# Three projections of a hybrid encoder layer: where the first one's column tiles and raw sums lie in SBUF, which queue loads them, and when its operands are split

## The chip, the cores and the metric

One core of one Trainium2 chip runs the whole layer. The metric is the device time of one execution in microseconds, the median of several runs; lower is better.

## The reference, cut to what matters

`x` is 512 tokens of 2048 channels. After RMSNorm, one input projection feeds two branches, an SSD scan and an attention over 16 heads. Each branch gives a 512 x 2048 array, `y` and `o`, and the layer ends with three 2048 x 2048 projections:

```python
o = bidir_attention(qn, qr, kn, kr, v) * jax.nn.silu(z_attn)
merged = jax.nn.sigmoid(g_ssm) * (y @ w_proj_ssm) + jax.nn.sigmoid(g_attn) * (o @ w_proj_attn)
return x + merged @ w_out            # float32 throughout, then a final RMSNorm
```

## The kernel before, in words

**Precision.** A float32 operand is split into a high part (`ACT` casts it to fp32r, L433) and a low part (`DVE` subtracts, L434); every product of two operands is three matmuls of 128 x 128 by 128 x 512 (high-high, low-high, high-low; L563, L564, L565).

**Strassen.** The projections `wps` (of `y`) and `wpa` (of `o`) use a 2 x 2 Strassen form, once for each half `cp` of the output columns. One half takes seven products, P1, P2, P5, P6, P3, P7, P4 in this order, of 48 matmuls each: four chunks `m` of weights (128 x 1024 f32, 512 KB each), and twelve matmuls a chunk. The operand side is one of x11, x12, S1, S2, S4, S3, x22 (`S1` to `S4` are sums of quarters of `y` or `o`); it is loaded raw in two halves of 512 KB (`raw_load`, L444, tile `xraw`) and split into a 16 KB-per-partition tile (`Ops.split`, `slot`). The weight side comes in tiles of three kinds: `wraw` (straight from `w`, three buffers, which the raw operand halves share), `X` and `Y` (four buffers each). X holds the "T1" column sums for P5, becomes X + Y for P6, and X + Y + `wraw` for P4; Y is P3's weight; "T3" sums, in Y buffers again, are P7's. T1 and T3 are made early by accumulating DMAs on POOL's queue.

**Who waits for whom.** A weight chunk is cast by ACT into `wh` and its rest written by DVE into `wl`, three buffers each, so the cast of chunk n waits until PE has done chunk n - 3. ACT, DVE, PE, and the queues of SP and POOL each work strictly in the order in which the scheduler of the program put them. PE's order is written by hand; those of the other engines follow the code order, moved forward by `high_priority(offset)` for loads (`LOAD_AHEAD`) and splits (`AHEAD`). `tc.keep_in_program_order` holds an instruction in code order.

**The stretch of the change.** In head 14 of the attention (`AH - 2`) `wps.head()` begins to be mixed into the heads: P1 and P2 of both halves of `wps` (called P1, P2, P1b, P2b) stand between the matmuls of heads 14 and 15. Before that the raw x11 and x12 of `y` are loaded and split into pool `xa`. When the last `pv` (probabilities by values, L168 to L170 on tile `op`) is written, pool `at` (attention tiles) closes and pool `xb` opens on the same memory, side "right", with `reuse_waits="tile"`: each new tile waits for the users of the bytes that it covers. In `xb` come five operand slots `opb` first, then four `Y`, then four `X`. The raw halves of S1 and S2 are put into `Y` tiles (loaded at L1477), the first T1 columns into `X` (L469), all on SP's queue. Then `wps.pair(0)`, `wps.pair(1)`, `wpa.pair(0)`, `wpa.pair(1)` run. `hooks` say after which product the next operand is loaded (`L`), split (`C`), or a step of the sums of `o` is issued on POOL's queue (`o_sums`: copies L1310, accumulates L1313). `done_ps` writes results to `ms_d` on POOL's queue (L1351), `fetch_ps` loads gates there (L1341).

Of the kernel before, what the change touches and what calls it, by code (L numbers as in the profile page):

```python
# [29 lines left out]
AH = 16  # L30
# [39 lines left out]
LOAD_AHEAD = 160  # L70


def build(tc, a):
    nc = tc.nc
    act, dve, pool, pe = nc.scalar, nc.vector, nc.gpsimd, nc.tensor
# [259 lines left out]
    class Fill:  # L335
# [43 lines left out]
    fill = Fill()  # L379
# [50 lines left out]

    def split_into(hi_, lo_, raw, sign=1):
        if sign == 1:
            act.copy(hi_, raw)  # L433
            dve.tensor_sub(lo_, raw, hi_.bitcast(F32))  # L434
# [12 lines left out]
    class Ops:  # L447
# [5 lines left out]
        def load(self, which):  # L453
            self.raws[which] = [raw_load(self.src[which], q) for q in range(2)]

        def split(self, which, op):
            for q, t in enumerate(self.raws.pop(which)):
                ks = slice(4 * q, 4 * q + 4)
                split_into(op[:, 0, ks], op[:, 1, ks], view4(t), -1 if which == "S2" else 1)
            self.view[which] = lambda s, j, i: op[:, s, j, i * P:(i + 1) * P]  # L460

    def w_load(t, w, cp, kh, cb, m):
# [1 line left out]
            nc.sync.dma_start(t, a[w][cp, kh, cb, m])  # L464
        return t

    def t_load(t, w, cp, name, m):
        with tc.high_priority(offset=LOAD_AHEAD):
            nc.sync.dma_start(t, t_d[w, cp, name][:, m * 1024:(m + 1) * 1024])  # L469
# [32 lines left out]
    def w_split(raw):  # L502
# [3 lines left out]
            split_into(h, l, raw)  # L506
        return h, l

    def w_tile(tag):
        with tc.high_priority(offset=LOAD_AHEAD):  # L510
            if tag == "w":
                return wp.tile([P, 1024], F32, tag="wraw", bufs=3, name="wraw")
            return cols.tile([P, 1024], F32, tag=tag, bufs=4, name=tag)

    def sum_tile(tag):

# [53 lines left out]
    class Strassen:  # L570
# [38 lines left out]

        def first(self, cp, name):  # L610
# [142 lines left out]
    cols = part_ = wx  # L753
# [505 lines left out]
    def scores(hd, t):  # L1259
        qh, ql, kh, kl, stack, zt = qks[hd]  # L1260
        tk = slice(t * P, (t + 1) * P)
        s = pa("s")
        pe.matmul(s, qh[:, tk], kh, start=True, stop=False)
        pe.matmul(s, qh[:, tk], kl, start=False, stop=False)
        pe.matmul(s, ql[:, tk], kh, start=False, stop=False)
        pe.matmul(s, stack[:, tk], kra, start=False, stop=False)
        pe.matmul(s, stack[:, tk], krb, start=False, stop=True)
        mx, nm, sm_ = (hi.tile([P, 1], F32, tag=n, bufs=4, name=n) for n in ("mx", "nm", "sm_"))
        dve.tensor_reduce(mx, s, AX.X, ALU.max)
        dve.tensor_scalar_mul(nm, mx, -SCALE)  # L1270
        pr = at_t("pr")
        act.activation(pr, s, AF.Exp, bias=nm, scale=SCALE, accum_out=sm_)
        dve.reciprocal(sm_, sm_)
        dve.tensor_scalar_mul(pr, pr, sm_)
        heads[hd][2][t] = pr
        if background and t == 1:
            pool.tensor_mul(pace, sm_, sm_)
            in_background(4)
# [107 lines left out]
    def o_sums(n, i=1):  # L1386
        return lambda: [tc.keep_in_program_order(f()) for f in o_late[i][n]]
# [27 lines left out]
    def some(n):  # L1415
        owed[0] += n
        owed[0] -= fill.run(owed[0])

    for hd in range(AH):
        pt_h = at.tile([P, TT, SEQ], F32R, tag="pt_h", bufs=2, name="pt_h")  # L1420
        pt_l = at.tile([P, TT, SEQ], F32R, tag="pt_l", bufs=2, name="pt_l")
        heads[hd] = (pt_h, pt_l, {})
        fill.until(("qk", hd))
        unit = 2.77 if hd < AH - 2 else 2
        scores(hd, 0)
        if hd:
            some(unit)
            trans(hd - 1, 3)
        some(2 * unit)
        scores(hd, 1)  # L1430
        some(3 * unit)
        if hd == AH - 2:
            fill.all()
            owed[0] = 0
            close_pool("ap")
            xa = part_ = open_pool("xa", reuse_waits="tile")
            for w in ("x11", "x12"):
                y_ops.load(w)
                y_ops.split(w, slot(w))
            kk = kp_  # L1440
            used.extend([0, 0, 3])
            fill.add("head", wps.head())
        if hd:
            pv(hd - 1)
        if hd == 12:
            for step in sums(o_d, slice(0, 1024)):
                for f in step:
                    f()
        trans(hd, 0)
        if hd == AH - 1:  # L1450
            o_sums(2, 0)()
        scores(hd, 2)
        some(3 * unit)
        trans(hd, 1)
        if hd == AH - 2:
            o_sums(0, 0)()
        some(2 * unit)
        scores(hd, 3)
        some(3 * unit)
        trans(hd, 2)  # L1460
        some(3 * unit)
        if hd >= AH - 2:
            o_sums((1, 3)[hd - AH + 2], 0)()
    some(8)
# [2 lines left out]
    pv(AH - 1, pb)  # L1467
    close_pool("at")
    xb = cols = open_pool("xb", side="right", reuse_waits="tile")
    xb.tile([P, 2, 8, 256], F32R, tag="opb", bufs=5, name="place")  # L1470
    for w, ahead_ in (("S1", LOAD_AHEAD), ("S2", 0)):
        if w == "S2":
            fill.all()
        with tc.high_priority(offset=ahead_):
            y_ops.raws[w] = [cols.tile([P, 1024], F32, tag="Y", bufs=4, name="xraw") for q in range(2)]
            for q in range(2):
                nc.sync.dma_start(y_ops.raws[w][q], yn_d[w][:, q * 1024:(q + 1) * 1024])  # L1477
# [160 lines left out]
```

## Time and profile before

| | |
|---|---|
| median of 3 runs (lowest, highest) | 2049.49 us (2048.11, 2053.45) |
| the profiled execution: its time, its span | 2056.61 us, 2054.8 us |
| mean granted TensorE clock in it | 0.985 |
| busy share of the span: PE, DVE, ACT, POOL | 96%, 71%, 47%, 15% |
| bytes moved by DMA | 378.56 MB, mean 184 GB/s |

The profile is one execution. A row of a timeline is: start in us, length, engine (SPq, POOLq or ACTq where its sequencer issues a DMA), line, operation, output<-inputs, shapes, count, and in brackets the idle time before it and what ended that. A row of the windows view gives, for each engine, the busy time in a stretch and the number of instructions that touch it (x), then the granted clock, the share of the 16 DMA engines that was busy, and GB/s. An unbroken stretch of PE in the Strassen products holds 44 to 45 matmuls in 10 us.

### The profile page before, as it was taken

Reading aid. Unit: us, or ns where it says so; the run is one execution under the profiler, and the core shown is the slowest. Engines: PE = TensorE matmul, PEld = TensorE weight load, DVE = VectorE, ACT = ScalarE, POOL = GpSimd, SP = SyncE. Lnnn points to the kernel's source line nnn. Section 1 sums busy time; section 2 is a strip of 40 time slices with the busy share of each in tenths; the row PEclk is TensorE's granted clock in tenths of the full one; section 3 lists DMA queues with packets and bytes.
Section 4 is the critical chain, followed back from the end, with each engine's and each line's share of the span. In section 5 each row is a group of like instructions: output and inputs, shape, how many; then the busy total and the mean of one; then the engine's idle time right before and its main releaser. Section 6 shows DMA issues by size and latency. Waiting matters only on the chain.

```text
span 2054.8 us, 24705 instructions
## 1 busy us (share of the span) xinstructions
PE 1970.9 (96%) x9074; PEld 1628.3 (79%) x9074; DVE 1466.0 (71%) x1946; ACT 968.1 (47%) x1352; POOL 318.0 (15%) x337
## 2 busy tenths in 40 slices
PE   6999999999999999999999989999999999999998
PEld 5878888888878787777788878888877777888886
DVE  7976676676669789799686667667576888776342
ACT  6444445444444656546456344444344454443232
POOL 0001011010032252342321101110010211100110
PEclk9999999999999999999999999999999999999999
DMA  5467657657457747687464856883377876865332
GB/s 196 164 179 202 171 127 194 183 120 188 134 174 193 222 142 207 195 237 230 145 189 146 241 161 180 211 220 95 85 207 257 293 251 258 264 227 169 109 117 82
DMA packets 166585, 378.56 MB, mean 184 GB/s; under 512 B 16001, under 2 KB 65281, under 8 KB 165889
## 3 DMA queue, kind: packets, MB, share of 16 engines
q1 hardware_dynamic: 104688, 238.33, 35.2%
q0 software_dynamic: 26944, 92.29, 20.5%
q10 hardware_dynamic: 34832, 46.38, 6.3%
q8 instruction: 71, 1.16, 0.2%
q14 instruction: 50, 0.40, 0.1%
HBM read 325.03 MB, written 98.04 MB: 206 GB/s over the span
## 4 chain that ended last, share of the span: by engine, by line
PE 72%; DVE 12%; DMA 7%; issue 5%; ACT 3%; POOL 1%; SPq 0%; ACTq 0%; DVEq 0%; POOLq 0%
PE P L564 10%; PE P L565 10%; PE P L563 10%; PE f L1507 3%; PE f L1508 3%; PE f L1506 3%; PE za L168 2%; PE za L169 2%; PE za L170 2%; PE xbc L168 2%; PE xbc L169 2%; DVE sum L1009 2%; PE xbc L170 2%; DVE wl L164 1%; DMA wraw<-wps 1%
## 5 line engine op out<-in xcount | busy, mean ns | idle before, releaser
L434 DVE TENSOR_TENSOR wl<-X,wh 128x1024 fp32r<-128x1024 f32 x152 | 185.4, 1223 | 82.4 <-ACT wh L433 81.7
L164 DVE TENSOR_TENSOR wl<-wraw,wh 128x1024 fp32r<-128x1024 f32 (+2 forms) x148 | 175.9, 1189 | 94.6 <-ACT wh L163 94.0
L433 ACT CAST wh<-X 128x1024 fp32r<-128x1024 f32 x152 | 159.4, 1053 | 155.6 <-PE P L565 135.8
L163 ACT CAST wh<-wraw 128x1024 fp32r<-128x1024 f32 (+2 forms) x150 | 145.0, 968 | 146.2 <-PE za L169 40.2
L434 DVE TENSOR_TENSOR wl<-wraw,wh 128x1024 fp32r<-128x1024 f32 x74 | 91.4, 1235 | 95.4 <-ACT wh L433 95.2
L434 DVE TENSOR_TENSOR wl<-Y,wh 128x1024 fp32r<-128x1024 f32 x80 | 98.0, 1225 | 76.4 <-ACT wh L433 76.4
L168 PE MATMUL xbc<-h_h,wh 128*128 128x512 f32 x384 | 152.4, 397 | 0.0
L170 PE MATMUL xbc<-h_h,wl 128*128 128x512 f32 x384 | 150.4, 392 | 0.0
L169 PE MATMUL xbc<-h_l,wh 128*128 128x512 f32 x384 | 150.3, 392 | 0.0
L564 PE MATMUL P<-wl,h_h 128*128 128x512 f32 x384 | 149.5, 389 | 0.0
L565 PE MATMUL P<-wh,h_l 128*128 128x512 f32 x384 | 149.5, 389 | 0.0
L563 PE MATMUL P<-wh,h_h 128*128 128x512 f32 x384 | 149.5, 389 | 0.0
L433 ACT CAST wh<-wraw 128x1024 fp32r<-128x1024 f32 x74 | 77.9, 1052 | 143.4 <-PE f L1508 68.6
L433 ACT CAST wh<-Y 128x1024 fp32r<-128x1024 f32 x80 | 83.9, 1051 | 113.9 <-PE P L565 91.4
L564 PE MATMUL P<-wl,S 128*128 128x512 f32 x288 | 112.5, 391 | 0.7 <-DVE wl L434 0.6
L563 PE MATMUL P<-wh,S 128*128 128x512 f32 x288 | 112.1, 389 | 0.0
L565 PE MATMUL P<-wh,S 128*128 128x512 f32 x288 | 112.1, 389 | 0.0
L168 PE MATMUL za<-h_h,wh 128*128 128x512 f32 x256 | 102.1, 399 | 0.0
L170 PE MATMUL za<-h_h,wl 128*128 128x512 f32 x256 | 100.7, 393 | 0.8 <-DVE wl L164 0.8
L169 PE MATMUL za<-h_l,wh 128*128 128x512 f32 x256 | 100.4, 392 | 0.0
L1009 DVE TENSOR_TENSOR_SCAN sum<-da,scn 128x512 f32<-128x512 f32 x64 | 87.3, 1382 | 0.0
L170 PEld LDWEIGHTS xbc<-h_h,wl 128*128 128x128 f32 x384 | 72.6, 189 | 15.6
(634 smaller groups left out, 5193.5 us busy)
## 6 DMA issues: line engine op xcount, KB each, us to landing
wraw<-wi SPq DMA_DIRECT2D x102, 512.0 KB, 4.1
T_wps<-wps POOLq DMA_DIRECT2D x32, 512.0 KB, 6.4
da<-da_d SPq DMA_DIRECT2D x64, 256.0 KB, 4.4
T_wpa<-wpa POOLq DMA_DIRECT2D x32, 512.0 KB, 9.5
wraw<-wo SPq DMA_DIRECT2D x32, 512.0 KB, 3.4
wraw<-wps SPq DMA_DIRECT2D x24, 512.0 KB, 4.8
xbc_d<-xbc ACTq DMA_DIRECT2D x24, 256.0 KB, 3.1
wraw<-wun SPq DMA_DIRECT2D x16, 384.0 KB, 3.1
```

The lines of the kernel that those rows point to most:

```text
L163: act.copy(h, raw)
L164: (dve if ahead[0] else pool).tensor_sub(l, raw, h.bitcast(F32))
L168: pe.matmul(out, wh, xh, start=start, stop=False)
L169: pe.matmul(out, wh, xl, start=False, stop=False)
L170: pe.matmul(out, wl, xh, start=False, stop=stop)
L433: act.copy(hi_, raw)
L434: dve.tensor_sub(lo_, raw, hi_.bitcast(F32))
L563: pe.matmul(bs[i], xh, wh, start=(j == 0), stop=False)
L564: pe.matmul(bs[i], xh, wl, start=False, stop=False)
L565: pe.matmul(bs[i], xl, wh, start=False, stop=(j == 7))
L1009: dve.tensor_tensor_scan(sums[dd], flat(da), mask, 0.0, ALU.add, ALU.mult)
L1506: pe.matmul(acc, mh, wh, start=(start and k == 0), stop=False)
```

## The change

1. **Pool `xb` has another order.** One slot (tag `opc`) first, then the four X tiles, then two tiles `Ya`, two tiles `Yb`, then four slots `opb`. X now covers the rotary query tile and the first `v_h` buffer, which the last `pv` does not use; `Yb` covers the first `v_l` buffer, also unused by then; `Ya` covers the second `v_h` buffer, which the last `pv` reads. S1's raw halves go to `Yb`, S2's to `Ya`.
2. **Eight loads change queue.** The first four T1 columns and the raw halves of S1 and S2 are issued on POOL's queue, not SP's.
3. **x12 of `y`** is loaded at the end of head 14 and split in head 15 code; it was loaded and split with x11.
4. **Operand splits of `o` move.** Each of x11, x12, S1, S2 of `o` is loaded and split one product later or more, its ACT cast pinned to code order (`CP`), and the steps of the sums of `o` are issued one or two products earlier.

```diff
 class Ops:
-        def split(self, which, op):
+        def split(self, which, op, in_order=False):
             for q, t in enumerate(self.raws.pop(which)):
                 ks = slice(4 * q, 4 * q + 4)
-                split_into(op[:, 0, ks], op[:, 1, ks], view4(t), -1 if which == "S2" else 1)
+                i = split_into(op[:, 0, ks], op[:, 1, ks], view4(t), -1 if which == "S2" else 1)
+                if in_order:
+                    tc.keep_in_program_order(i)          # i is the ACT cast
...
+    def col_tile(tag, name, dt=F32):
+        if tag == "Y" and cols is xb:
+            n_cols[0] += 1
+            return cols.tile([P, 1024], dt, tag=("Yb", "Ya")[(n_cols[0] - 1) // 2 % 2], bufs=2, name=name)
+        return cols.tile([P, 1024], dt, tag=tag, bufs=4, name=name)
...
+    def place(shape, name):
+        n = n_places[0] % 5
+        n_places[0] += 1
+        return xb.tile(shape, F32R, tag="opb" if n else "opc", bufs=4 if n else 1, name=name)
...
     wps = Strassen("wps", y_ops, -1, done_ps, fetch_ps, {
-        (0, "P5"): [C(y_ops, "S4"), L(y_ops, "S3"), o_sums(5, 0), o_sums(0)],
-        (0, "P6"): [C(y_ops, "S3"), L(y_ops, "x22"), o_sums(1)], (0, "P3"): [C(y_ops, "x22"), o_sums(2)],
-        (0, "P7"): [L(o_ops, "x11"), o_sums(3)], (0, "P4"): [C(o_ops, "x11"), L(o_ops, "x12"), o_sums(4)],
-        (1, "P5"): [C(o_ops, "x12"), L(o_ops, "S1"), o_sums(5)], (1, "P6"): [C(o_ops, "S1"), L(o_ops, "S2")],
-        (1, "P3"): [C(o_ops, "S2")], (1, "P7"): [L(o_ops, "S4")], (1, "P4"): [C(o_ops, "S4"), L(o_ops, "S3")]})
+        (0, "P5"): [C(y_ops, "S4"), L(y_ops, "S3"), o_sums(1)],
+        (0, "P6"): [C(y_ops, "S3"), L(y_ops, "x22"), o_sums(2)], (0, "P3"): [C(y_ops, "x22"), o_sums(3)],
+        (0, "P7"): [o_sums(4)], (0, "P4"): [L(o_ops, "x11"), o_sums(5)],
+        (1, "P5"): [CP(o_ops, "x11"), L(o_ops, "x12")], (1, "P6"): [CP(o_ops, "x12"), L(o_ops, "S1")],
+        (1, "P3"): [CP(o_ops, "S1"), L(o_ops, "S2")], (1, "P7"): [CP(o_ops, "S2"), L(o_ops, "S4")],
+        (1, "P4"): [CP(o_ops, "S4"), L(o_ops, "S3")]})
     wpa = Strassen("wpa", o_ops, -1, done_pa, fetch_pa, {
-        (0, "P1"): [C(o_ops, "S3"), L(o_ops, "x22")], (0, "P5"): [C(o_ops, "x22")],
+        (0, "P1"): [CP(o_ops, "S3"), L(o_ops, "x22")], (0, "P5"): [CP(o_ops, "x22")],
...
         scores(hd, 1)
+        if hd == AH - 1:
+            y_ops.split("x12", slot("x12"))
         some(3 * unit)
         if hd == AH - 2:
 ...
-            for w in ("x11", "x12"):
-                y_ops.load(w)
-                y_ops.split(w, slot(w))
+            y_ops.load("x11")
+            y_ops.split("x11", slot("x11"))
...
         some(3 * unit)
+        if hd == AH - 2:
+            y_ops.load("x12")
         if hd >= AH - 2:
             o_sums((1, 3)[hd - AH + 2], 0)()
...
     xb = cols = open_pool("xb", side="right", reuse_waits="tile")
-    xb.tile([P, 2, 8, 256], F32R, tag="opb", bufs=5, name="place")
-    for w, ahead_ in (("S1", LOAD_AHEAD), ("S2", 0)):
-        if w == "S2":
-            fill.all()
-        with tc.high_priority(offset=ahead_):
-            y_ops.raws[w] = [cols.tile([P, 1024], F32, tag="Y", bufs=4, name="xraw") for q in range(2)]
-            for q in range(2):
-                nc.sync.dma_start(y_ops.raws[w][q], yn_d[w][:, q * 1024:(q + 1) * 1024])
-        if w == "S1":
-            wps.first_columns(0)
-        C(y_ops, w)()
+    place([P, 2, 8, 256], "place")
+    wps.first_columns(0, pool)
+    for tag in ("Ya", "Yb"):
+        cols.tile([P, 1024], F32, tag=tag, bufs=2, name="place")
+    with tc.high_priority(offset=LOAD_AHEAD):
+        for w in ("S1", "S2"):
+            y_ops.raws[w] = [col_tile("Y", "xraw") for q in range(2)]
+            for q in range(2):
+                pool.dma_start(y_ops.raws[w][q], yn_d[w][:, q * 1024:(q + 1) * 1024])
+    CP(y_ops, "S1")()
+    fill.all()
+    CP(y_ops, "S2")()
     L(y_ops, "S4")()
     o_sums(4, 0)()
+    o_sums(5, 0)()
+    o_sums(0)()
     run(wps.pair(0, True))
```

PE's order is the same in both. What moves on the other engines, at three places (the number behind a name is a buffer's; `_213` and `_214` are S1 and S2 of `y`, `_216`, `_215`, `_212` are S4, S3, x22 of `y`, and `_217`, `_218` are x11, x12 of `o`):

SP's queue before, from the last head's value tile to the first pair (eleven `wraw` of P1, P2, P1b and P2b's first, then the S1 and T1 loads, then P2b's other three weights):

```order
L1226 DMA zt<-za_d_92 128x512
L464 DMA wraw<-wps 128x1024 x11
L1477 DMA xraw<-yn_S_213 128x1024
L469 DMA X<-T_wps_201 128x1024 x4
L1477 DMA xraw<-yn_S_213 128x1024
L464 DMA wraw<-wps 128x1024 x3
L1477 DMA xraw<-yn_S_214 128x1024 x2
L464 DMA Y<-wps 128x1024 x4
```

Three of P2b's four weights stand behind six transfers of 512 KB. SP's queue now, at the same place:

```order
L1239 DMA zt<-za_d_92 128x512
L467 DMA wraw<-wps 128x1024 x13
L467 DMA Y<-wps 128x1024
L445 DMA xraw<-yn_S_216 128x1024 x2
L467 DMA Y<-wps 128x1024
L445 DMA xraw<-yn_S_215 128x1024
L467 DMA Y<-wps 128x1024
```

All weights of P2b now stand in one row behind P1's, with nothing between; the Y loads are interleaved with the raw halves of S4 and S3.

POOL's queue now, from the last sum of `o` in the heads to the first results of `wps` (before, the first row was followed at once by `ms_d`):

```order
L1326 DMA o_S_222<-o_x_220 128x512
L472 DMA X<-T_wps_201 128x1024
L1507 DMA xraw<-yn_S_213 128x1024
L472 DMA X<-T_wps_201 128x1024 x3
L1507 DMA xraw<-yn_S_213 128x1024
L1507 DMA xraw<-yn_S_214 128x1024 x2
L1376 DMA ms_d_0_177<-p_13096 128x512
```

The eight loads stand between the last sum and the first result.

ACT before, from P3's weight casts (Y) to the eviction of the second half's P5 (`p`); `x__13529` is x22 of `y`, `x__13714` and `x__13814` are x11 and x12 of `o`:

```order
L433 CAST x__13529<-xraw 128x1024
L433 CAST wh<-Y 128x1024 x6
L433 CAST wh<-X 128x1024
L433 CAST x__13714<-xraw 128x1024
L433 CAST wh<-X 128x1024
L433 CAST x__13714<-xraw 128x1024
L433 CAST wh<-X 128x1024
L433 CAST x__13814<-xraw 128x1024
L433 CAST wh<-X 128x1024 x2
L433 CAST x__13814<-xraw 128x1024
L433 CAST wh<-X 128x1024 x5
```

Between two casts of P4's weights stands each time the cast of an operand half. ACT now, the same stretch and on to P3's casts of the second half (`x__13532` is x22 of `y`, `x__13808` and `x__13887` x11 and x12 of `o`):

```order
L433 CAST x__13532<-xraw 128x1024
L433 CAST wh<-Y 128x1024 x7
L433 CAST wh<-X 128x1024 x10
L539 COPY p_13804<-P_13718 128x512
L539 COPY p_13806<-P_13719 128x512
L433 CAST wh<-X 128x1024
L433 CAST x__13808<-xraw 128x1024 x2
L433 CAST wh<-X 128x1024
L433 CAST x__13887<-xraw 128x1024
L433 CAST wh<-Y 128x1024
L433 CAST x__13887<-xraw 128x1024
```

The four casts of `o`'s operands leave the row of P4's and P5's weight casts and now stand behind the second half's P5, the last of them behind the first Y cast of the second half's P3.

More of the change, by code (lines that the diff above doesn't have):

```diff
@@ L432, in split_into @@
         if sign == 1:
-            act.copy(hi_, raw)
+            i = act.copy(hi_, raw)
             dve.tensor_sub(lo_, raw, hi_.bitcast(F32))
         else:
-            act.activation(hi_, raw, AF.Copy, scale=-1.0)
+            i = act.activation(hi_, raw, AF.Copy, scale=-1.0)
             dve.scalar_tensor_tensor(lo_, raw, -1.0, hi_.bitcast(F32), ALU.mult, ALU.subtract)
+        return i
     def view4(t):
@@ L465, in w_load, with t_load @@
         return t
-    def t_load(t, w, cp, name, m):
+    def t_load(t, w, cp, name, m, queue=nc.sync):
         with tc.high_priority(offset=LOAD_AHEAD):
-            nc.sync.dma_start(t, t_d[w, cp, name][:, m * 1024:(m + 1) * 1024])
+            queue.dma_start(t, t_d[w, cp, name][:, m * 1024:(m + 1) * 1024])
         return t
@@ L507, in w_split @@
         return h, l
+    xa = xb = None
+    n_cols = [0]
+    def col_tile(tag, name, dt=F32):
[3 more added lines that the diff above has]
+        return cols.tile([P, 1024], dt, tag=tag, bufs=4, name=name)
     def w_tile(tag):
@@ L512, in w_tile @@
                 return wp.tile([P, 1024], F32, tag="wraw", bufs=3, name="wraw")
-            return cols.tile([P, 1024], F32, tag=tag, bufs=4, name=tag)
+            return col_tile(tag, tag)
     def sum_tile(tag):
@@ L598, in r_sum, with first_columns, columns @@
                 dve.scalar_tensor_tensor(out, x, -1.0, y, ALU.mult, ALU.subtract)
-        def first_columns(self, cp):
-            self.ahead[cp] = [self.columns(w_tile("X"), cp, m) for m in range(4)]
-        def columns(self, t, cp, m):
+        def first_columns(self, cp, queue=nc.sync):
+            self.ahead[cp] = [self.columns(w_tile("X"), cp, m, queue) for m in range(4)]
+        def columns(self, t, cp, m, queue=nc.sync):
             if self.made:
-                return t_load(t, self.w, cp, "T1", m)
+                return t_load(t, self.w, cp, "T1", m, queue)
             return w_load(t, self.w, cp, 0, 0, m)
@@ L1320, in build @@
             f()
-    xa = xb = None
+    n_places = [0]
+    def place(shape, name):
+        n = n_places[0] % 5
+        n_places[0] += 1
+        return xb.tile(shape, F32R, tag="opb" if n else "opc", bufs=4 if n else 1, name=name)
     def slot(which):
-        op_pool, tag, n = (xa, "opa", 2) if which in ("x11", "x12") else (xb, "opb", 5)
-        return op_pool.tile([P, 2, 8, 256], F32R, tag=tag, bufs=n, name=f"{which}_")
+        if which in ("x11", "x12"):
+            return xa.tile([P, 2, 8, 256], F32R, tag="opa", bufs=2, name=f"{which}_")
+        return place([P, 2, 8, 256], f"{which}_")
     y_ops, o_ops = Ops(yn_d), Ops(o_d)
@@ L1335, in C, with CP @@
         return lambda: ops.split(w, slot(w))
+    def CP(ops, w):
+        return lambda: ops.split(w, slot(w), True)
     fetched = {}
@@ L1378, in f @@
         def f():
-            t = mg[b] = xb.tile([P, 2, 4, SEQ], F32R, tag="opb", bufs=5, name="m")
+            t = mg[b] = place([P, 2, 4, SEQ], "m")
             for q, r_ in enumerate(m_raw.pop(b)):
@@ L1525, in last_load @@
             if i == 0:
-                last_w["op"] = xb.tile([P, 2, 2, 1024], F32R, tag="opb", bufs=5, name="keep")
+                last_w["op"] = place([P, 2, 2, 1024], "keep")
             h, l = (last_w["op"][:, i, s_] for s_ in range(2))
         else:
-            h, l = (xb.tile([P, 1024], F32R, tag=tag, bufs=4, name="keep") for tag in "XY")
+            h, l = (col_tile(tag, "keep", F32R) for tag in "XY")
         split_into(h, l, raw)
```

2 lines of the change are left out of this document (1 added, 1 removed).

## The prediction, made before the changed kernel ran

> **What bounds the kernel now.** I read the page first: PE is busy for nearly the whole span, and the chain that ended last is mostly PE.
>
> ```profile
> span 2054.8 us, 24705 instructions
> PE 1970.9 (96%) x9074; PEld 1628.3 (79%) x9074; DVE 1466.0 (71%) x1946; ACT 968.1 (47%) x1352; POOL 318.0 (15%) x337
> PE 72%; DVE 12%; DMA 7%; issue 5%; ACT 3%; POOL 1%; SPq 0%; ACTq 0%; DVEq 0%; POOLq 0%
> ```
>
> PE's matmuls and their order don't change, so the change can win or lose only time in which PE stands or runs at a lower clock. Up to 1490 us the queues are as they were; what counts is the stretch from there to the end of `wps`. The windows view cuts it so that stalled and unbroken stretches stand apart (per engine busy us and count, then clock, DMA share, GB/s).
>
> ```profile
> core 0: us, PE busy (x) PEld busy (x) DVE busy (x) ACT busy (x) POOL busy (x), PEclk, DMA share, GB/s
> 1490.00:1510.00 20.00, 20.00 (x99) 16.60 (x98) 12.77 (x27) 8.61 (x18) 3.68 (x5) 1.00 0.76 202
> 1510.00:1530.00 20.00, 15.69 (x58) 11.46 (x57) 15.48 (x26) 10.67 (x17) 1.37 (x2) 0.83 0.85 246
> 1530.00:1560.00 30.00, 30.00 (x144) 24.78 (x143) 19.17 (x34) 14.05 (x25) 0.80 (x1) 1.00 0.45 135
> 1570.00:1590.00 20.00, 15.71 (x62) 12.29 (x61) 11.62 (x10) 9.94 (x10) 0.00 (x0) 0.91 0.87 334
> 1590.00:1610.00 20.00, 20.00 (x90) 16.56 (x89) 19.07 (x20) 13.09 (x14) 4.62 (x8) 1.00 0.68 210
> 1610.00:1630.00 20.00, 17.78 (x76) 13.86 (x75) 15.89 (x18) 7.88 (x8) 1.68 (x2) 1.00 0.97 336
> 1640.00:1660.00 20.00, 16.14 (x59) 12.51 (x57) 15.51 (x17) 8.09 (x8) 3.09 (x5) 0.83 0.77 283
> 1700.00:1710.00 10.00, 7.04 (x28) 4.72 (x27) 7.05 (x8) 6.73 (x7) 3.21 (x6) 1.00 1.03 417
> 1710.00:1740.00 30.00, 30.00 (x134) 24.85 (x133) 28.07 (x27) 15.87 (x18) 2.14 (x4) 1.00 0.56 222
> ```
>
> An unbroken 20 us hold 99 matmuls in the heads (0.202 us each) and 90 in the pairs (0.222 us). What a stretch lacks of that is its loss, half clock included: 41 in the heads, 41 x 0.202 = 8.3 us; at 1570, 28 x 0.222 = 6.2; at 1610, 14 = 3.1; at 1640, 31 = 6.9; at 1700, 45 - 28 = 17 = 3.8. Together 28.3 us. After 1710 nothing is lost. So the change can bring at most 28 us, 1.4%.
>
> **Part 1, the first weights of P1 (8.3 us).** P1's first weights wait for the buffers that the raw x11 and x12 hold.
>
> ```profile
> 1508.72 2.00 ACT L433 CAST x__12693<-xraw 128x1024 fp32r<-128x1024 f32 x2
> 1513.73 1.59 SPq L464 DMA_DIRECT2D wraw<-wps  x2
> 1518.47 1.04 ACT L433 CAST wh<-wraw 128x1024 fp32r<-128x1024 f32 x1 [1.01 <-DMA wraw<-wps]
> 1519.56 0.50 PE L563 MATMUL P<-wh,x__12693 128*128 128x512 f32 x1 [2.32 <-ACT wh L433]
> 1520.82 0.80 PE L564 MATMUL P<-wl,x__12693 128*128 128x512 f32 x1 [0.76 <-DVE wl L434]
> ```
>
> With x12 later, two weight loads follow x11's halves directly and their casts stand ahead of x11's, so both waits of PE go: 2.32 + 0.76 = 3.1 us. The half clock goes with them: 0.83 over 20 us is 17% of 20 = 3.4 us. The other 8.3 - 6.5 = 1.8 us are waits for softmax pieces behind x11's split on ACT and DVE, which stays. x12's two casts (1.0 us each, as x11's in the first row) and its subtractions now fall between the weight casts of P1, with x12's second raw half waiting for x11's buffer; I expect 1.5 us of new waits there for a scaled score row ahead of a transpose. Gain 6.5 - 1.5 = 5.0 us, ends 3 and 8.
>
> The Trainium skill ("TensorE: Matmul & The Clock Gate", Part 1: The HAM clock gate) states that the clock falls to half after an idle window of some 3.4 us. By that rule the 2.32 and 0.76 us above would not have caused the half clock, and its 3.4 us would stay: the sum would be 3.4 us smaller. The trace shows the half clock right behind them, so the sum goes by the trace.
>
> **Part 2, the first pair's loads on POOL's queue (6.2 us).** At P2b everything arrives at once.
>
> ```profile
> 1530.12 0.80 POOL L1313 DMA_DIRECT2D o_S<-o_x  x1 [5.58 <-DMA o_S<-o_S]
> 1559.94 0.37 SPq L1477 DMA_DIRECT2D xraw<-yn_S  x1
> 1560.40 2.56 SPq L469 DMA_DIRECT2D X<-T_wps  x4
> 1561.58 0.60 POOL L1351 DMA_DIRECT2D ms_d<-p  x1 [30.65 <-DVE p L1350]
> 1563.89 11.92 DMA wraw<-wps
> 1574.53 1.04 ACT L433 CAST S__13064<-xraw 128x1024 fp32r<-128x1024 f32 x1 [3.17 <-DMA xraw<-yn_S]
> 1575.88 1.04 ACT L433 CAST wh<-wraw 128x1024 fp32r<-128x1024 f32 x1 [0.31 <-DMA wraw<-wps]
> 1576.98 0.49 PE L563 MATMUL P2b<-wh,x__12702 128*128 128x512 f32 x1 [3.53 <-ACT wh L433]
> ```
>
> P2b's second weight takes 11.92 us to land behind six 512 KB transfers, and ACT stands 3.17 us for S1 in front of it. Now the six leave SP. On POOL they come behind the sum at 1530.12, where POOL then idles 30.65 us; their tiles lie over bytes that the last heads no longer read, so they issue from about 1531 on, at 0.8 us each. The DMA engines are 45% busy there at 135 GB/s; they moved 336 GB/s at 0.97, so 30 us have room for 30 x 201 = 6.0 MB, and six times 0.524 MB is 3.1. What they could delay are P2's and P1b's weights, which are loaded some 10 us before use. S2's two raw halves wait for the last `pv` (PE, about 1556); behind them on POOL stand only `ms_d` of P2 at 1561.58 and its gates. SP loses eight issues of 0.4 us and no longer holds P2b's weights. Gain 6.0 of 6.2, ends 4 and 6.2. If POOL could not issue them before 1560, the 6.2 would stay.
>
> The Trainium skill ("DMA: Bandwidth & Descriptors", Issuing engines are not separate DMA queues) says that all queues run on the same 16 engines and another issuing engine saves only issue time. By that rule alone, with the loads still at 1560, this part would bring nothing and the sum 6.0 us less. The rows show that it is the place in time that changes, and no run so far shows the two apart.
>
> **Part 3, x22 ahead of P3 (3.1 us).** ACT stands for x22's second half with P3's weights queued behind it.
>
> ```profile
> 1603.01 2.77 SPq L444 DMA_DIRECT2D xraw<-yn_x  x2
> 1614.13 1.05 ACT L433 CAST x__13529<-xraw 128x1024 fp32r<-128x1024 f32 x1 [4.91 <-DMA xraw<-yn_x]
> ```
>
> This half was issued at about 1605.5 and took 8.7 us. Now S4 and S3 are cast during P5, but DVE's subtraction of S4's second half and of S3 stands behind the `wl` of P6's chunks, and those subtractions free x22's buffers. Working it through with PE unbroken, x22 issues at about 2.6 and 5 us after P6's start (before: 4.3 and 6.8), and only one Y cast, not two, stands ahead of its second half. With a landing of 4.7 us (the shortest row of part 4) nothing is lost; with 8.7 again some 3 us. DVE is full there (19.07 of 20 us in 1590 to 1610). I take 2.0 lost, gain 1.1, ends -1 and 3.
>
> **Part 4, operands of `o` out of P4 (6.9 us).** The two halves of x12 of `o` hold up P4's weight casts.
>
> ```profile
> 1634.01 9.76 DMA xraw<-o_x
> 1636.38 0.39 SPq L444 DMA_DIRECT2D xraw<-o_x  x1
> 1643.79 1.04 ACT L433 CAST x__13814<-xraw 128x1024 fp32r<-128x1024 f32 x1 [6.10 <-DMA xraw<-o_x]
> 1648.97 1.04 ACT L433 CAST x__13814<-xraw 128x1024 fp32r<-128x1024 f32 x1 [2.24 <-DMA xraw<-o_x]
> ```
>
> In the new order no operand cast stands between P4's: gain 6.9, ends 5 and 6.9. Three 512 KB loads (x12's second half, S1) also leave this saturated stretch. Against it: DVE now adds the last two `wraw` into X back to back ahead of P7's second `wl`, and the last of them waits for its buffer, 0.7 us; and x12's second half is now issued when x11's first is split, 4.8 us after P5 of the second half, while ACT reaches it 2.9 us later, with P3's second Y cast behind it and slack for a landing of 5.5 us; 0.7 us. Landings of half a megabyte in this trace go from 4.71 to 11.92 us.
>
> ```profile
> 1513.73 4.71 DMA wraw<-wps
> 1682.93 5.22 DMA wraw<-wps
> ```
>
> **Part 5, S4 and S3 of `o` ahead of the second P4 (3.8 us).** Here too ACT stands for operands with weights behind.
>
> ```profile
> 1700.03 1.05 ACT L433 CAST S__14164<-xraw 128x1024 fp32r<-128x1024 f32 x1 [5.45 <-DMA xraw<-o_S]
> 1705.09 1.05 ACT L433 CAST S__14251<-xraw 128x1024 fp32r<-128x1024 f32 x1 [3.06 <-DMA xraw<-o_S]
> ```
>
> Now S4's casts stand behind five X casts and S3's behind the next product. But S2's halves keep two of three buffers until P7, so P4's third and fourth `wraw` are issued only when S2's halves are split, in P7, some 6 us before PE wants the third X; with the 5.22 us landing above, the addition and the cast behind it, that X is ready 0.9 us late. I take 2.0 lost, gain 1.8, ends -2 and 3.8.
>
> The sums of `o` on POOL move from under P6 to P4 to P2b to P7; the copies and accumulates are the same in number, none is waited for by the products of `y`, and they cost nothing but DMA share, which is counted in parts 3 to 5.
>
> **Sum.** 5.0 + 6.0 + 1.1 + 6.9 - 0.7 - 0.7 + 1.8 = 19.4 us. The profiled execution took 2056.6 us and would take 2037.2; the median of the runs is 7.1 us under it, so I forecast 2049.5 - 19.4 = 2030 us. The ends of the parts added are 3 + 4 - 1 + 5 - 0.7 - 0.7 - 2 = 7.6, and 27.9 with the two new waits at nothing.
>
> **Rivals.**
> - *Everything clears.* All landings are near 4.8 us because the burst at 1560 is gone and the sums are spread. Then 26 to 28 us go: 2022. For it: every stall stands in a stretch with a DMA share of 0.85 to 1.03. Against it: P3 and P7 still load seven half megabytes each in 11 us, 337 GB/s, about what full engines moved (336). Chance 0.15.
> - *DMA stays the bound.* Stalls in P3, P7 and both P4 come back, because the bytes are the same and the stretch is shorter. Parts 3 and 5 bring nothing, P7 and P4 lose 4 us: 19.4 - 1.1 - 1.8 - 4 = 12.5, or 2037. Chance 0.22.
> - *The loads do not move.* POOL's queue reaches them only behind a late sum, or P2's weights suffer as P2b's did: 2030 + 6 = 2036. The 30.65 us speak against it. Chance 0.05.
> - *Slower: pinned casts wait in order.* Each pinned operand's second half is issued only when a buffer frees and ACT then stands for it. At P3, P7, P4 of the second half and at two products of `wpa` that is a stall of the landing less 5.5 us. At 9.8 us landing (the row at 1634) it is 5 x 4.3 = 21 us, and with half the time as half clock 5 x 1.7 = 8.5 more; parts 1 and 2 and P4 bring 18, so 12 us slower: 2061. It decides from landings of about 8.5 us at all five. Chance 0.04.
>
> **Numbers.** The forecast itself, 2024 to 2036, has the remaining 0.54. Range 2021 to 2041: it leaves out the slow side's tail and little below. 0.3% is 6.1 us, about what a measurement of this kernel can tell from no change (the three runs span 5.3). Faster by more than that: all of the 0.54, 0.15 and 0.05, and 0.17 of the 0.22 (its rest ends above 2043.4), 0.91, less a little for the tails, 0.90; within 0.3%: 0.06; slower: 0.04.
>
> **What would show it.** T1 columns and S1 issued by POOL between 1530 and 1540, and no wait of P2b for `wh` over 1 us; P1's first matmul directly behind the score matmuls, at clock 1.0; ACT without a wait for `xraw` of `o` among P4's casts; a wait left at P3 or the second P4 of 1 to 3 us. Wrong would be: a wait of ACT of over 4 us for the x12 half of `o` in the second half's P3, late P2 weights behind POOL's loads, or a loss in `wpa`.

## The result, and the profile after

The changed kernel took 2040.26 us (median of 5 runs, 2034.87 to 2043.42), the kernel before 2049.49 (2048.09 to 2058.72). The ratio is 0.9935, 95% interval 0.9913 to 0.9957: faster by 0.65%. Run again later beside other kernels it gave 0.9946 (0.9930 to 0.9961).

The first lines of the page of the changed kernel:

```profile
span 2033.1 us, 24719 instructions
PE 1955.8 (96%) x9074; PEld 1619.0 (80%) x9074; DVE 1465.7 (72%) x1946; ACT 967.4 (48%) x1352; POOL 324.7 (16%) x345
PE 72%; DVE 14%; DMA 6%; issue 4%; ACT 3%; POOL 1%; SPq 0%; ACTq 0%; DVEq 0%; POOLq 0%
```

The two profiled spans are 21.7 us apart, more than the medians, because the profiled execution of before lies 7.1 us above its median and that of the changed kernel (2034.87 us) 5.4 under it. At the first matmul of the last `pv` ahead of P1 the changed kernel is 10.4 us ahead already, in work that both do alike (1500.86 against 1511.26 us; other profiles with the changed kernel's order reach it at 1503 and at 1511). So the stretch from there on is compared: to the first matmul of `wpa` it took 188.25 us, before 199.80. That is 11.55 us less; behind it nothing differs (347.05 and 358.63 us to the end of `wpa`). The next lines are the windows view of the changed kernel, with the columns of the one shown of before.

```profile
1499.60:1519.60 20.00, 17.51 (x84) 13.42 (x83) 17.86 (x33) 12.88 (x22) 2.47 (x4) 1.00 0.81 250
1555.70:1566.60 10.90, 10.90 (x50) 9.01 (x49) 9.12 (x9) 9.25 (x10) 0.00 (x0) 1.00 0.86 294
1566.00:1577.00 11.00, 11.00 (x50) 9.12 (x49) 10.17 (x11) 6.12 (x6) 1.07 (x2) 1.00 0.34 137
1588.00:1599.00 11.00, 11.00 (x50) 9.10 (x49) 10.71 (x12) 4.80 (x5) 1.68 (x2) 1.00 1.00 336
1599.00:1610.00 11.00, 6.91 (x23) 5.25 (x22) 7.17 (x9) 2.14 (x3) 1.54 (x3) 0.76 0.99 349
1628.00:1638.00 10.00, 10.00 (x46) 8.29 (x45) 9.56 (x11) 4.70 (x5) 3.10 (x5) 1.00 0.24 87
1671.00:1682.00 11.00, 7.15 (x29) 5.38 (x29) 7.04 (x7) 3.04 (x3) 1.07 (x2) 0.90 0.97 388
1682.00:1689.00 7.00, 7.00 (x23) 5.49 (x22) 6.04 (x9) 3.14 (x3) 2.14 (x4) 0.67 0.93 269
```

The heads run at clock 1.00 (0.83 before), and P2b (second row) is unbroken. But two stretches have holes in PE and a lower clock: 1599, which is P7 of the first half, and 1671, which is P4 of the second. In both the DMA engines are full, while at 1566 and 1628, three products before and two behind the first hole, they move 137 and 87 GB/s.

What PE waited for in P7 is seen in DVE's timeline:

```profile
1597.60 1.23 DVE L434 TENSOR_TENSOR wl<-Y,wh 128x1024 fp32r<-128x1024 f32 x1
1600.58 1.23 DVE L674 TENSOR_TENSOR X<-X,wraw 128x1024 f32<-128x1024 f32 x1 [1.75 <-DMA wraw<-wps]
1604.02 1.23 DVE L674 TENSOR_TENSOR X<-X,wraw 128x1024 f32<-128x1024 f32 x1 [2.21 <-DMA wraw<-wps]
1605.16 1.22 DVE L434 TENSOR_TENSOR wl<-Y,wh 128x1024 fp32r<-128x1024 f32 x1
```

The row at 1605.16 is the `wl` of P7's second chunk. Its `wh` was there at 1599; it stood behind two additions that P4 needs only a product later, each of which waited for a `wraw`. In P4 of the second half the additions themselves are late (ACT's timeline, then two rows of the chain):

```profile
1677.16 1.04 ACT L433 CAST wh<-X 128x1024 fp32r<-128x1024 f32 x1 [6.37 <-DVE X L674]
1679.56 1.99 ACT L433 CAST wh<-X 128x1024 fp32r<-128x1024 f32 x2 [1.35 <-DVE X L674]
```

```profile
1595.24 8.76 DMA wraw<-wps
1669.65 8.54 DMA wraw<-wps
```

Both `wraw` took over 8.5 us to land, where the rows shown in the prediction had 4.71 and 5.22.

### The profile page after: what moved, and what is told of

It reads as the page before. It is cut to its first block, busy times and chain, and to the rows that moved or that the text cites. A ratio compares the mean times of both kernels' runs of the same rounds, so it can differ in the third digit from the quotient of the medians.

```text
span 2033.1 us, 24719 instructions
## 1 busy us (share of the span) xinstructions
PE 1955.8 (96%) x9074; PEld 1619.0 (80%) x9074; DVE 1465.7 (72%) x1946; ACT 967.4 (48%) x1352; POOL 324.7 (16%) x345
## 4 chain that ended last, share of the span: by engine, by line
PE 72%; DVE 14%; DMA 6%; issue 4%; ACT 3%; POOL 1%; SPq 0%; ACTq 0%; DVEq 0%; POOLq 0%
PE P L577 10%; PE P L578 10%; PE P L576 10%; PE f L1539 3%; PE f L1540 3%; PE f L1538 3%; PE za L168 2%; PE za L169 2%; PE za L170 2%; PE xbc L168 2%; DVE sum L1022 2%; PE xbc L169 2%; PE xbc L170 2%; DVE wl L164 2%; DMA wraw<-wps 1%
```

## The experiments

Each product is read as the time from its first matmul to the next product's; one without a stall is 10.88 us. "Heads" goes from the first matmul of the last `pv` ahead of P1 to P1b, "all" from there to the end of `wpa`. "P4-P6'" are P4 and the second half's P5 and P6 (32.64 without a stall), "wpa P1-P2" the first four products of `wpa` (43.52).

| kernel | heads | P2b | P3 | P7 | P4-P6' | second P4 | wpa P1-P2 | all | ratio to before |
|---|---|---|---|---|---|---|---|---|---|
| before | 48.43 | 17.24 | 13.96 | 10.88 | 39.87 | 15.02 | 43.52 | 358.63 | |
| changed | 43.98 | 10.89 | 10.87 | 17.65 | 32.64 | 17.83 | 43.52 | 347.05 | 0.9935 |
| e8 (as e1) loads on SP | 44.37 | 20.48 | 12.71 | 12.12 | 32.64 | 16.53 | 43.52 | 352.43 | 0.9980 (e1) |
| e2 old places of `o` | 43.98 | 10.89 | 11.01 | 16.38 | 34.67 | 14.61 | 43.52 | 347.20 | 0.9940 |
| e3 additions late | 44.40 | 10.88 | 10.88 | 10.88 | 36.14 | 18.18 | 44.26 | 345.43 | 0.9943 |
| e4 sums later | 44.24 | 10.88 | 11.24 | 18.11 | 32.64 | 19.42 | 43.52 | 353.09 | 0.9967 |
| e5 S2 later | 46.80 | 10.88 | 11.12 | 18.22 | 32.64 | 10.88 | 47.64 | 348.55 | 0.9930 |
| e6 all later | 44.40 | 10.88 | 10.88 | 11.53 | 36.54 | 10.88 | 60.30 | 355.55 | 0.9974 |
| e7 x12 early | 47.26 | 10.88 | 10.88 | 16.37 | 32.64 | 18.23 | 43.52 | 349.49 | 0.9963 |
| e9 e3 and e5 | 44.98 | 10.88 | 10.88 | 11.30 | 34.88 | 10.88 | 44.93 | 338.46 | 0.9903 |
| e10 changed again | 44.49 | 10.88 | 10.91 | 16.40 | 32.65 | 17.96 | 43.52 | 346.65 | 0.9946 |
| e11 without adds | 43.54 | 10.88 | 10.94 | 13.85 | 32.64 | 17.60 | 43.52 | 343.51 | (one run) |

The ratios carry about 0.002 either way, 4 us, so single steps are read from the product times, and the ratio only says whether they add up. A product time is that of one profiled execution: in the four kernels with the changed kernel's order from P1b to P7 (changed, e5, e7, e10) P7 took 16.4 to 18.2 us, so differences under 2 us there say nothing.

**e1 and e8: the eight loads on SP's queue.**

```diff
-    wps.first_columns(0, pool)
+    wps.first_columns(0)
...
-                pool.dma_start(y_ops.raws[w][q], yn_d[w][:, q * 1024:(q + 1) * 1024])
+                nc.sync.dma_start(y_ops.raws[w][q], yn_d[w][:, q * 1024:(q + 1) * 1024])
```

> The changed kernel, with the eight loads (four T1 columns, S1, S2) on SP's queue again; tiles and places in the code as in the change. SP's order then has them behind P2b's first weight and ahead of its other three. Theory (the place in time decides, and POOL's queue is what gives it): SP reaches them only when the buffers of P1b's weights come free, some 15 us later than POOL does, so P2b's weights again land behind 4 MB: P2b stalls 4 to 6 us (none now), and the time is some 5 us above the changed kernel, ratio to the kernel before 0.996 to 0.998. Rival (the free tiles alone do it, another issuing queue saves only issue time): P2b stalls under 1 us, ratio 0.993 to 0.995 as the changed kernel.

Its ratio is 0.9980 (0.9966 to 0.9995), as the theory had it. Its product times come from e8, another execution of the same kernel:

> The first run's kernel again (the eight loads on SP's queue), one look, for its profile. Theory: X's first column is issued by SP some 15 us later than by POOL, P2b's wraw stand behind, and P2b takes 15 to 17 us (10.88 now). Rival: P2b takes under 12 us.

SP's timeline in e8, a row of its chain, and POOL's timeline in the changed kernel:

```profile
1538.73 11.70 SPq L467 DMA_DIRECT2D wraw<-wps  x4
1550.54 0.37 SPq L472 DMA_DIRECT2D X<-T_wps  x1
1556.60 3.61 SPq L467 DMA_DIRECT2D wraw<-wps  x3
```

```profile
1556.60 12.43 DMA wraw<-wps
```

```profile
1520.13 0.96 POOL L472 DMA_DIRECT2D X<-T_wps  x1
1521.24 2.21 POOL L472 DMA_DIRECT2D X<-T_wps  x3
1541.67 1.05 POOL L1507 DMA_DIRECT2D xraw<-yn_S  x2 [17.70 <-PE op L170]
```

The tiles are the same and equally free. SP comes to the first column 44.6 us behind the `pv` (1550.54 - 1505.91), POOL 19.3 us (1520.13 - 1500.86), because SP stands 11.70 us on weights whose buffers are not free. The next of P2b's `wraw`, behind the eight loads, then takes 12.43 us to land, and P2b 20.48 us. Freeing the tiles alone doesn't help; the theory holds, with a larger price in P2b than the 15 to 17 us expected. Of its 9.6 us only 5.4 are left at the end (352.43 - 347.05), mostly because P7 stalls 5.5 us less. DVE has the same order there as in the changed kernel, two additions ahead of the second `wl`, but the last `wraw` lands sooner:

```profile
1612.28 5.45 DMA wraw<-wps
```

**e2: parts 1 to 3 of the change alone**, with loads, splits and sums of `o` as before: the removed rows of the hooks in the diff of the change stand again, and

```diff
     o_sums(4, 0)()
-    o_sums(5, 0)()
-    o_sums(0)()
```

> The changed kernel with the loads, splits and sums of o where they were before (parts 1 to 3 of the change alone). Theory (moving o's operands only moved the stalls): P4 and the second P4 stall again for operand halves of o (6 and 3 us), but P7 of the first pair (6.8 us now) and the 6.9 us of the second P4 go down; in sum 0 to 4 us under the changed kernel, ratio to the kernel before 0.991 to 0.994. Rival (the move of o's operands earned its 6.9 us): about 5 us above the changed kernel, ratio 0.995 to 0.997.

0.9940 (0.9922 to 0.9959), and 347.20 us against 347.05: the move of `o`'s operands is worth nothing. Its stalls stand in other products: P7 loses 5.5 us and the second half's P5 to P7 1.1, 0.8, 1.2 and 0.8, where the changed kernel loses 6.8 in P7 and 3.2 us more in the second P4. The theory's sum came nearly true, but not its places: P4 does not stall again for operand halves (10.96 us), and P7 loses as much as in the changed kernel's other profile (5.5). DVE's timeline in e2 shows why P7 does:

```profile
1604.81 1.23 DVE L674 TENSOR_TENSOR X<-X,wraw 128x1024 f32<-128x1024 f32 x1 [2.29 <-DMA wraw<-wps]
1607.26 1.23 DVE L674 TENSOR_TENSOR X<-X,wraw 128x1024 f32<-128x1024 f32 x1 [1.23 <-DMA wraw<-wps]
1608.40 1.22 DVE L434 TENSOR_TENSOR wl<-Y,wh 128x1024 fp32r<-128x1024 f32 x1
```

The two additions stand ahead of P7's second `wl` here too, with the operands of `o` in their old places. That order of DVE came with parts 1 to 3, not with part 4; which of the three brings it isn't shown.

**e3: P7's last two additions behind its `wl`.**

```diff
-                t4(m, w_load(w_tile("w"), w, cp, 1, 0, m))
+                raw = w_load(w_tile("w"), w, cp, 1, 0, m)
+                t4(m, raw) if m < 2 else tc.keep_in_program_order(dve.tensor_add(X[m], X[m], raw))
```

> The changed kernel with one edit in P7: the third and fourth addition of wraw into X are held in code order, so DVE does them behind the wl of P7's chunks. Theory (P7 waits because the addition that waits for the last wraw stands ahead of the second chunk's wl): P7 of the first pair takes 11 to 12.5 us (17.65 now), that is 5 to 6.5 us less, ratio to the kernel before 0.990 to 0.992 if P4 doesn't take it back. Rival (DMA is the bound, T3's weights are late as well): P7 stays above 15 us, or P4 takes back what P7 wins, because X's third and fourth tile come late; ratio 0.993 to 0.995.

P7 takes 10.88 us: its 6.8 us were DVE's order alone, not late T3 weights. But 3.5 us come back in P4 to P6'. ACT's timeline in e3 shows it at P5 of the second half, for T1 columns:

```profile
1630.08 1.04 ACT L433 CAST wh<-X 128x1024 fp32r<-128x1024 f32 x1 [7.41 <-DMA X<-T_wps]
1631.94 1.05 ACT L433 CAST wh<-X 128x1024 fp32r<-128x1024 f32 x1 [0.82 <-DMA X<-T_wps]
```

The whole stretch gained 1.6 us (1.2 against e10), and the ratio (0.9943, 0.9924 to 0.9961) can't tell that from nothing. So both theories had a half.

**e4: sums of `o` issued from P4 on.**

```diff
-        (0, "P6"): [C(y_ops, "S3"), L(y_ops, "x22"), o_sums(2)], (0, "P3"): [C(y_ops, "x22"), o_sums(3)],
-        (0, "P7"): [o_sums(4)], (0, "P4"): [L(o_ops, "x11"), o_sums(5)],
+        (0, "P6"): [C(y_ops, "S3"), L(y_ops, "x22")], (0, "P3"): [C(y_ops, "x22")],
+        (0, "P7"): [], (0, "P4"): [L(o_ops, "x11"), o_sums(2)],
...
         (the second half's P5, P6 and P3 get o_sums(3), o_sums(4), o_sums(5))
```

> The changed kernel with steps 2 to 5 of the sums of o's second column half issued behind P4, and in P5, P6, P3 of the second half (before: behind P6 to P4 of the first). Theory of order on DVE: the last wraw of P7 lands 1 to 2 us earlier (8.76 us now), P7 still stalls 3 to 6 us, ratio 0.992 to 0.994. Rival (the accumulating DMAs fill the engines and are the cause): the landing falls to about 5 us, P7 stalls under 2 us, ratio 0.990 to 0.991. Against both: S2 and S4 of o could come late in the second half's P3 and P7 behind POOL's gates; then the second P4 stalls more than 7 us.

Neither, but the third case that was named: P7 takes 18.11 us with a landing of 8.74, and S2 comes later (its second raw half is issued 2.3 us ahead of the second half's P7, against 4.5 in the changed kernel), and the second P4 takes 19.42 us; 0.9967 (0.9954 to 0.9980). The landing in P7 is as slow without the later steps of the sums beside it.

**e11: the accumulating DMAs of those sums left out.**

```diff
-        return lambda: [tc.keep_in_program_order(f()) for f in o_late[i][n]]
+        return lambda: [tc.keep_in_program_order(f()) for f in (() if i and n % 2 else o_late[i][n])]
```

> The changed kernel without the accumulating DMAs of the sums of o's second column half (the copies stay, the sums are left out, so S1 to S4 of o hold only copies there). Theory (order on DVE and buffers make the two stalls; the accumulates are 1 of some 15 MB): P7 still stalls by 4 us or more and the second P4 by 5 or more. Rival (accumulating DMAs slow the loads beside them): P7 stalls under 2 us; the second P4, behind which no sum runs, stays as it is.

One row of its chain:

```profile
1597.86 7.24 DMA wraw<-wps
```

The landing falls to 7.24 us (8.76 and 8.17 in the two profiles of the changed kernel), and P7's stall to 3.0 us (6.8 and 5.5), between the two expectations; the second P4 stays (17.60). More than half of what P7 gains is that the clock stays at 1.00 behind the shorter hole (2.56 us; 4.09 and 3.58 there). In e3, with all sums in place, that landing was 7.67 us, so this one execution leaves open whether the accumulates cost P7 anything.

**e5: S2, S4, S3 and x22 of `o` one product later.**

```diff
-        (1, "P3"): [CP(o_ops, "S1"), L(o_ops, "S2")], (1, "P7"): [CP(o_ops, "S2"), L(o_ops, "S4")],
-        (1, "P4"): [CP(o_ops, "S4"), L(o_ops, "S3")]})
+        (1, "P3"): [CP(o_ops, "S1")], (1, "P7"): [L(o_ops, "S2")],
+        (1, "P4"): [CP(o_ops, "S2"), L(o_ops, "S4")]})
...
-        (0, "P1"): [CP(o_ops, "S3"), L(o_ops, "x22")], (0, "P5"): [CP(o_ops, "x22")],
+        (0, "P1"): [CP(o_ops, "S4"), L(o_ops, "S3")], (0, "P5"): [CP(o_ops, "S3"), L(o_ops, "x22")], (0, "P6"): [CP(o_ops, "x22")],
```

> The changed kernel with S2, S4, S3 and x22 of o each loaded and split one product later (S2 is loaded in the second half's P7 and split in its P4). Theory (S2's raw halves hold two of the three wraw buffers, so the last two wraw of the second P4 are issued too late): the second P4 takes 11 to 13 us (17.8 now), nothing comes back in the attention projection, ratio to the kernel before 0.990 to 0.992. Rival (full DMA engines, 0.97 there, are what makes the last wraw late): the second P4 stays above 15 us, ratio 0.993 to 0.995.

The second P4 takes 10.88 us. Its last `wraw` is now issued 10.9 us ahead of it, 1.6 in the changed kernel: S2's raw halves in the `wraw` buffers were the cause of the stall. 4.1 us come back in `wpa`'s first four products, 2.5 of them in its P5. ACT's timeline in e5 there:

```profile
1706.62 1.05 ACT L433 CAST wh<-X 128x1024 fp32r<-128x1024 f32 x1 [3.50 <-DMA X<-T_wpa]
1710.35 1.05 ACT L433 CAST wh<-X 128x1024 fp32r<-128x1024 f32 x1 [2.68 <-DMA X<-T_wpa]
```

The ratio (0.9930, 0.9904 to 0.9956) leaves both open. The theory's "nothing comes back" failed. In this profile the heads took 2.8 us more than in the changed kernel, with the same order there.

**e6: e3, and every operand of `o` one product later still.**

```diff
-        (0, "P7"): [o_sums(4)], (0, "P4"): [L(o_ops, "x11"), o_sums(5)],
...
+        (0, "P7"): [o_sums(4)], (0, "P4"): [o_sums(5)],
+        (1, "P5"): [L(o_ops, "x11")], (1, "P6"): [CP(o_ops, "x11"), L(o_ops, "x12")],
+        (1, "P3"): [CP(o_ops, "x12")], (1, "P7"): [L(o_ops, "S1")],
+        (1, "P4"): [CP(o_ops, "S1"), L(o_ops, "S2")]})
...
+        (0, "P1"): [CP(o_ops, "S2"), L(o_ops, "S4")], (0, "P5"): [CP(o_ops, "S4"), L(o_ops, "S3")], (0, "P6"): [CP(o_ops, "S3"), L(o_ops, "x22")], (0, "P2"): [CP(o_ops, "x22")],
```

> The late additions of the third run (P7's third and fourth addition behind its wl) and every operand of o one product later still: x11 is loaded in the second half's P5 and split in P6, S2 is split after the attention projection's P1. Theory (each stall left is a load that meets a burst, and moving 1 MB of x11 out of the first P4 and S2 out of the second P7 thins both): P7 of the first pair and the second P4 take 11 to 12.5 us, the waits of P4, P5 and P6 for T1 columns in the third run (3.5 us) go below 2, ratio 0.986 to 0.989. Rival (the bytes only come back elsewhere): over 4 us of new stalls, in the second half or in the attention projection, ratio 0.991 to 0.994.

0.9974 (0.9955 to 0.9992). P7 and the second P4 are nearly clean and T1 columns are still waited for, but `wpa`'s P6 and P2 lose 4.2 and 12.5 us. SP's timeline there:

```profile
1711.80 2.59 SPq L445 DMA_DIRECT2D xraw<-o_x  x2
1716.21 24.29 SPq L467 DMA_DIRECT2D wraw<-wpa  x5
```

x22's halves now hold two of the three `wraw` buffers while P2 wants them for its weights, so P2's loads go one by one for 24 us. The rival's new stalls came, larger than it had them (its ratio was 0.991 to 0.994), and by buffers, not by bytes.

**e7: x12 of `y` loaded and split beside x11**, as before.

```diff
-            y_ops.load("x11")
-            y_ops.split("x11", slot("x11"))
+            for w in ("x11", "x12"):
+                y_ops.load(w)
+                y_ops.split(w, slot(w))
```

> The changed kernel with x12 of y loaded and split beside x11, as before. Theory: P1's first weights wait again for x12's raw buffers, and the heads from the last but one pv to P1b take 47 to 49 us (43.98 now, 48.43 before); ratio to the kernel before 0.995 to 0.997. Rival (the 4.5 us came from elsewhere, the loads on POOL's queue or noise of the half clock): the heads stay at 44 to 45 us, ratio as the changed kernel, 0.992 to 0.995.

Two rows of PE's timeline in e7, and a row of its windows view:

```profile
1510.84 0.49 PE L576 MATMUL P<-wh,x__12693 128*128 128x512 f32 x1 [2.31 <-ACT wh L433]
1512.10 0.50 PE L577 MATMUL P<-wl,x__12693 128*128 128x512 f32 x1 [0.77 <-DVE wl L434]
```

```profile
1510.00:1530.00 20.00, 18.39 (x81) 14.95 (x82) 14.69 (x27) 10.46 (x18) 5.39 (x9) 0.91 0.93 264
```

The same two waits as before the change (2.32 and 0.76), again with half clock behind them (0.91), heads of 47.26 us, ratio 0.9963 (0.9943 to 0.9983). That is 2.8 to 3.3 us more than in the two profiles of the changed kernel. The time alone would not show the cause, since e5 takes 46.80 us with x12 late; the two waits do.

**e9: e3 and e5 together, and e10, the changed kernel beside it.**

> The third and the fifth run's edits together: P7's third and fourth addition behind its wl, and S2, S4, S3, x22 of o one product later. Theory (the two waits are separate and each leaves a smaller one behind, where the next loads meet full engines): P7 and the second P4 take 10.9 to 11.5 us, some 3.5 us of waits stay in P4 to P6 and some 4 in the attention projection's first products; from the last but one pv to the end of wpa 340 to 344 us (347.05 in the changed kernel, 358.63 before), ratio to the kernel before 0.989 to 0.992, and 4 to 6 us under the changed kernel on the same chip. Rival (the stalls are set by the bytes of the whole stretch, so that what is taken out of P7 and P4 comes back in full): 346 to 349 us, the same time as the changed kernel.

> The changed kernel itself, beside the run above on the same chip: ratio to the kernel before 0.992 to 0.996, P7 16 to 18.5 us, the second P4 17 to 18.5.

e9 took 2032.16 us (2025.11 to 2036.98), ratio 0.9903 (0.9879 to 0.9926); the changed kernel on the same chip 2038.74 us. That is 6.6 us by medians and 8.2 by the stretch (338.46 against 346.65), more than the 4 to 6 expected. Alone, e3 brought 1.2 us of it (346.65 - 345.43) and e5, counted from P1b because of its heads, 0.4 (302.16 - 301.75). But 1.8 us of what e5 took stand in P7, which its edit doesn't touch, so that its own gain is rather 2 us. Two rows of the windows view of e9, over P3 and most of P7 and over P7 and P4 of the second half:

```profile
1592.00:1612.00 20.00, 20.00 (x90) 16.51 (x89) 17.73 (x21) 8.26 (x9) 4.39 (x7) 1.00 1.02 354
1665.00:1685.00 20.00, 20.00 (x89) 16.54 (x89) 19.48 (x24) 9.81 (x10) 5.34 (x10) 1.00 0.99 389
```

PE is unbroken at clock 1.00 while the DMA engines are as full as in the changed kernel. So full engines alone did not stop PE here; what stopped it was who stood behind the late loads. Waits of 2.2 us are left in P4-P6', and of 1.4 in `wpa`'s first products.

## Why the prediction was right in sign and too large in size

The time lies in the range, but 0.7 us under its upper end and outside the 2024 to 2036 us of the forecast itself; of 19.4 us forecast, 11.55 came in the stretch and 9.2 in the medians. That it still fell into the range is partly luck: the terms missed by up to 6 us, in both directions.

- **Part 1 (5.0 us).** Right: the heads took 4.45 us less, without a wait of PE for P1's first weights and at clock 1.00. The new waits for score rows, put at 1.5 us, came too (0.83 and 0.68 us). e7 puts some 3 us of the gain on x12's place, by the two waits that come back. The rest is within what the heads differ by where their order is the same (43.5 to 46.8 us). The half clock went with the waits, and came back with them in e7; in e5 it came at 1530 us without them, behind a wait of 1.86 us for a score row, so this part of the gain isn't there in every execution. By the Trainium skill's rule ("TensorE: Matmul & The Clock Gate", Part 1: The HAM clock gate) an idle window of some 3.4 us is needed; the two waits in e7, 2.31 and 0.77 us, lie under that, so here the measured rows decide (the last section counts them).
- **Part 2 (6.0).** Right: P2b took 6.35 us less, with the loads issued about when forecast, and e8 shows that POOL's queue is what does it. By the Trainium skill's rule ("DMA: Bandwidth & Descriptors", Issuing engines are not separate DMA queues) another issuing queue saves only issue time. With tiles and place in the code the same, P2b took 20.48 us from SP and 10.89 from POOL: the engines are shared, but each queue waits in its own order.
- **Part 3 (1.1).** Better: P3 took 3.1 us less, the upper end of the term. x22's halves were issued 2.8 and 5.1 us after P6's start, as worked out (2.6 and 5), and landed in 4.5 and 3.5 us, under the 4.7 us at which it had no loss.
- **Part 4 (6.9 less 0.7 and 0.7).** P4 and the half clock of P5 behind it took 7.2 us less, as forecast, but only 2.0 us of that belong to the move: e2, with the operands in their old places and P7 about as late, has the other 5.2 too (34.67 against 39.87 us in P4-P6'). The failed step is the 0.7 us put on P7's second `wl`. The mechanism was named, two additions ahead of that `wl`, the last waiting for its buffer, though e2 shows that this order came with parts 1 to 3. Its size was 6.8 us. The prediction names no landing for this term; beside it stand rows of 4.71 and 5.22 us. With the last `wraw` issued when it was, a landing of 5.4 us would have left a hole of 0.7 us in PE; it was 8.76, and the hole 4.09 us, before the matmul at 1606.43. The hole then brought half clock with it, which the term doesn't have. In e8, with the same order on DVE and a landing of 5.45 us, P7 lost 1.2 us. Why the landing grew is argued, not shown alone: P3 without its stall starts P7 3.1 us earlier against the same loads, and e8, where P3 still stalls by 1.8 us, fits that. Nor was 4.71 us the shortest landing of half a megabyte in the trace of before, as the prediction has it: its page has a median of 3.4 us for the weights of `wo`. The 0.7 us for x12 in the second P3 didn't come.
- **Part 5 (1.8).** Wrong sign: the second P4 lost 2.8 us more than before. The step was again the landing, 8.54 us where 5.22 was taken, with half clock behind the stall (0.67); that S2's halves keep two of three buffers was named, and without it in e5 the whole stall is gone.

4.45 + 6.35 + 3.09 + 7.23 - 6.77 - 2.81 = 11.54. The rival "DMA stays the bound", with 2037 us, comes nearest. It had P7 and P4 lose 4 us; they lost more, and P3 and the first P4 didn't stall. e2 bears out its sense: parts 4 and 5 together bring nothing, and all that the change won is in parts 1 to 3. The rival "Everything clears" read the rows too evenly: the one at 1640 us has a DMA share of 0.77, not 0.85 or more.

## What to carry to other kernels

When the engines move all they can, the landing time to put into a sum is that of the full stretch (8 to 9 us here), not that of an emptier one, above all if the step ahead has just lost a stall of its own. Look then for what stands behind a late load: an addition needed a product later, ahead of a weight needed now, cost 6.8 us, and an operand parked in the weights' buffers cost 7.0; each was undone by moving a few instructions. Undo such waits together, since the next one can take back most of what the first alone wins (some 1 and 2 us alone, 8.2 together, the single gains from one profile each).

## What the runs showed of the hardware

Issuing a transfer from another queue moved it 25 us ahead where SP stood on buffers (44.6 against 19.3 us behind the `pv`). The landing of 512 KB took 4.71 us in the heads of before and 12.43 us in e8, behind eight such loads issued within 6 us. Without the accumulating DMAs of four sums, 1 of some 13 MB in that stretch, one landing in P7 took 7.24 us, where the same one took 7.67 to 9.46 in the other profiles but e8's; whether accumulates cost more than their bytes, or that run was lucky, stays open.

The half clock can be counted. In the profiles of before, changed and e2 to e11 each of its stretches is 3.41 or 6.83 us long, and within a profile they start whole multiples of 3.41 us apart. In the spans of that grid, some 6700, half clock never followed a span at full clock in which PE stood less than 1.4 us, and always followed one in which it stood more than 1.95 us; between the two both happen. Two spans of e7 and two of e3 show it:

```profile
1509.82:1513.24 3.42, 1.63 (x6) 1.15 (x7) 2.02 (x3) 1.50 (x2) 0.00 (x0) 1.00 1.01 346
1513.24:1516.65 3.41, 3.41 (x12) 2.73 (x11) 1.64 (x3) 1.95 (x3) 1.38 (x2) 0.50 0.78 237
```

```profile
1630.37:1633.78 3.41, 1.85 (x7) 1.31 (x8) 2.59 (x3) 1.80 (x2) 0.00 (x0) 1.00 0.68 278
1633.78:1637.20 3.42, 3.42 (x17) 2.83 (x16) 3.42 (x4) 2.11 (x2) 0.00 (x0) 1.00 0.02 8
```

PE stood 1.79 us in the first span of e7, and the clock fell to 0.50; in e3 it stood 1.56 us, and the clock stayed at 1.00. So waits of PE shorter than 3.4 us cost half clock behind them, if they take up about half of one such span.
